# Scores as two full-row passes, one weight-product burst per head pair, and gate sums ahead of their matmuls, in a two-block transformer kernel on one core

## The chip, the cores and the metric

The kernel runs as one program on one core of a Trainium2 chip. The metric is the device time of one execution in microseconds; the kernel before takes 2135.71 us, the median of three runs (2135.44 to 2136.05). Everything is computed in 32-bit floats; a long linear product is made of three matmuls on operands split into a high part (rounded to TensorE's reduced 32-bit format, `F32R`) and a low part (the remainder).

## The reference

512 tokens of width 1024 pass through two blocks. The first block has two layers of: a norm, one wide projection, sparse attention, a short convolution branch, gates, and an MLP of width 4096. In the attention, an indexer scores all keys for each query with four small heads, the best 128 (`topk`) keys are kept, and eight heads of width 64 attend to those:

```python
logits = jnp.einsum('bthd,bsd->bths', iqb, ikf)                 # indexer, 4 heads of 64
score = jnp.einsum('bths,bth->bts', jax.nn.relu(logits), iwb) * IDX_SCALE
_, idx = lax.top_k(score, topk)
s = jnp.einsum('bthd,btkhd->bthk', qb, kg) * scale              # 8 heads of 64
p = jax.nn.softmax(s, axis=-1)
return jnp.einsum('bthk,btkhd->bthd', p, vg)
```

The second block has a dilated attention of eight heads of width 64 beside an mLSTM with four heads (whose input and forget gates are eight columns of the input projection, `ig` and `fg`), and a SwiGLU of width 2816. Its modulation vector comes from a small product with `c`.

## The kernel before, in words

Activations lie as features x tokens, in tiles of 128 x 512. `linear` (L188) makes an output tile from three matmuls per 128 input rows (L230 to L232): high weights by high input, high weights by low input, low weights by high input. `linear_tok` (L240, matmuls L260 to L262) is the same with tokens on the partitions. Weights are fetched by SyncE's queue in pieces of up to 1 MB, and each unit of 128 x 1024 is split by ScalarE (L171) and VectorE (L172), two units ahead of use (`Prog.run`, L56).

The program is a list of steps in the order written. Attention steps are spread between the pieces of a projection by `interleave` (L85): in the first block's layers between those of the second gate, in the second block between those of the mLSTM projections. From the written order each engine's own order is planned when the program is built: an instruction written earlier goes first if its inputs and buffers are there by the planner's estimate. An engine then executes its order strictly; on TensorE matmuls start in that order. All 128 x 512 intermediate tiles come from one pool of 60 buffers (`slot`, tag `g`, L123); TensorE's output banks are four for linear layers (`mm`), three for attention and small products (`at`), one for attention outputs (`ot`).

Attention runs over 16 units: four head pairs times four query tiles `i` of 128 (`attn_pieces`, L417). For step `t` it writes the scores of unit `t`, the transposes of unit `t - 1` and the weight product of unit `t - 2`; the operands of the next pair (`parts`, L400) are written at a pair's second unit.

- `scores` (L344): per head a bank gets two matmuls with (i + 1) x 128 columns, at least 256. The first (L350) uses all 128 rows: the high query part stands twice, and the key operand has high and low part one above the other, so it gives qh kh + qh kl. The second (L351) uses 64 rows: ql kh. VectorE then adds the bias and takes the maximum (L354), ScalarE takes exp (L359) and scales (L362).
- `transp` (L365): TensorE transposes the weights tile by tile (L370); VectorE copies the first head's out of the bank (L373), ScalarE the second's (L375).
- `product` (L378): for a query tile, (i + 1) x 2 matmuls (L385); the two heads use 64 columns of the array each. A full 32-bit product (no `F32R`) is two instructions per matmul in the trace, so L385 has 480 of them in three attentions.

The index scores (`iscore`, L580) are made of a full-row and a 64-row matmul in the same way (L587, L588), 12 in each of the first block's layers. The gate columns of the second block (`gates0`, L1005) are made in two parts: VectorE adds the high and low part of four input tiles (L1014), and four matmuls with 32 columns of the array each (L1016), one strip for each tile, follow; the second part adds to the first. The first part is written after six, the second after eleven of the 16 pieces of the V projection. `qk1` has four matmuls of that shape too (L963).

Of the kernel before, what the change touches and what calls it, by code (L numbers as in the profile page):

```python
# [15 lines left out]
P = 128  # L16
# [11 lines left out]
# columns of the packed vectors  # L28
# [10 lines left out]
# columns of the constants  # L39
# [8 lines left out]
class Prog:  # L48
    """A list of emission steps; weight units are fetched and split ahead of use."""
# [35 lines left out]
def interleave(a, b):  # L85
    """Spread the pieces of b evenly between the pieces of a."""
    out = []
    na, nb = len(a), len(b)
    j = 0
    for i, x in enumerate(a):  # L90
        out.extend(x)
        while j < nb and (j + 1) * na <= (i + 1) * nb:
            out.extend(b[j])
            j += 1
    while j < nb:
        out.extend(b[j])
        j += 1
    return out
# [3 lines left out]
def blocks_kernel(ctx: ExitStack, tc: tile.TileContext, a: dict, out: bass.AP, stop=None):  # L102
# [35 lines left out]
    # ---------------------------------------------------------------- constants  # L138
# [16 lines left out]
    # ---------------------------------------------------------------- weights  # L155
# [25 lines left out]
    def halves(ch):  # L181
        """Units of at most 256 columns over all K tiles of a chunk."""
# [5 lines left out]
    def linear(W, row0, kts, c0, widths, xs, evac, parts_=1):  # L188
        """Output tiles (features x tokens) of W[row0:, c0:].T @ x; pieces of emission items.

        kts: K tiles per step; widths: columns of each output tile; xs: K tile -> (hi, lo);
        evac(j, psum, tokens) is emitted after the last product of output tile j; parts_: the
        tokens go through the group in that many parts, one after the other.
        """
# [45 lines left out]
    def linear_tok(W, c0, xs, evac):  # L240
        """Output tiles (tokens x 512 features)."""
# [37 lines left out]
    # ---------------------------------------------------------------- shared state  # L279
# [9 lines left out]
    def prep(key, j, gcol, sq=True):  # L289
        """x_j * g in two parts, and its part of the sum of squares."""  # L290
# [18 lines left out]
    def rstd(key):  # L309
        """1/sqrt(mean + eps) of every token, on all partitions."""  # L310
# [10 lines left out]
    def refine(y, v, t):  # L321
        """One Newton step of y = v ** -0.5."""
# [15 lines left out]
    # ---------------------------------------------------------------- attention  # L338
    def attn_unit(pair, i, stacks, V, bias, O):
        """Steps of one (head pair, query tile): scores, transposed weights, product."""  # L340
# [3 lines left out]
        def scores():  # L344
            qs, ql, ks = stacks[pair]
            WM = max(W, 2 * P)
            for hh in range(2):
                r = slice(64 * hh, 64 * hh + 64)
                ps = atbank()
                pe.matmul(ps[:, :WM], qs[hh][:, i * P : (i + 1) * P], ks[hh][:, :WM], start=True, stop=False)  # L350
                pe.matmul(ps[:, :WM], ql[r, i * P : (i + 1) * P], ks[hh][r, :WM], start=False, stop=True)  # L351
# [13 lines left out]
        def transp():  # L365
            for hh in range(2):
# [9 lines left out]
                st["T", hh] = pt  # L376

        def product():  # L378
            if i == 0:
                S["ops"] = otbank()  # L380
            ops = S["ops"]
            for j in range(i + 1):
                for hh in range(2):
                    h = 2 * pair + hh
                    pe.matmul(  # L385
                        ops[64 * hh : 64 * hh + 64, i * P : (i + 1) * P],
                        V(j)[:, 64 * h : 64 * h + 64],
                        st["T", hh][:, j * P : (j + 1) * P],
                        start=j == 0,
                        stop=j == i,  # L390
                    )
            st.pop(("T", 0))
            st.pop(("T", 1))
            if i == NT - 1:
                O[pair] = hilo(ops)
                stacks.pop(pair)

        return scores, transp, product

    def parts(q32, k32):  # L400
        """Two-part operands of a head pair: per head [qh; qh] and [kh; kl] (or [kl; kh]), and ql."""
        qs = [slot(F32R), slot(F32R)]
        ks = [slot(F32R), slot(F32R)]
        ql = slot(F32R)
        qh = slot(F32R)
        act.copy(qh, q32)
        dve.tensor_sub(ql, q32, qh.bitcast(F32))
        for hh in range(2):
            r = slice(64 * hh, 64 * hh + 64)
            o = slice(64 - 64 * hh, 128 - 64 * hh)  # L410
            act.copy(ks[hh][r], k32[r])
            dve.tensor_sub(ks[hh][o], k32[r], ks[hh][r].bitcast(F32))
            act.copy(qs[hh][r], q32[r])
            act.copy(qs[hh][o], q32[r])
        return qs, ql, ks

    def attn_pieces(q, k, V, bias, O):  # L417
        """Software-pipelined pieces over all (pair, query tile)."""
# [7 lines left out]
        us = [attn_unit(a_, i, stacks, V, bias, O) for a_ in range(4) for i in range(NT)]  # L426
# [3 lines left out]
        for t in range(n + 2):  # L430
# [7 lines left out]
            if t >= 2:  # L438
                p.append(("do", us[t - 2][2]))
# [4 lines left out]
    # ================================================================ block 1  # L444
    START = [1, 1, 2, 4]

    def dma_in(chunks):
        def f():
            act.activation(small(1, "nm"), epsc, AF.Sqrt)
            # keeps the PE array busy, so that its clock is up when the first operands arrive  # L450
# [24 lines left out]
    def layer1(l, nextprep):  # L475
# [6 lines left out]
        # ---- indexer projections  # L482
# [3 lines left out]
        def evA(j, ps, cs):  # L486
            if j < 2:
                t = slot()
                rope(ps, P, [t])
                ql = slot(F32R)  # L490
                qh = slot(F32R)
                act.copy(qh, t)
                dve.tensor_sub(ql, t, qh.bitcast(F32))
                for hh in range(2):
                    qs = slot(F32R)
                    r = slice(64 * hh, 64 * hh + 64)
                    act.copy(qs[0:64], t[r])
                    act.copy(qs[64:128], t[r])
                    iq[2 * j + hh] = (qs, ql)
# [981 lines left out]
```

## Time and profile before

| | |
|---|---|
| median of three runs | 2135.71 us (2135.44 to 2136.05) |
| profiled execution, first to last instruction | 2133.5 us, 2.2 us under the median; no other time of that execution is given |
| TensorE busy | 2126.5 us (100%), 9944 matmul instructions |
| VectorE busy | 1250.9 us (59%) |
| ScalarE busy | 864.9 us (41%) |
| GpSimd busy | 1.6 us |
| DMA | 215.25 MB, mean 101 GB/s |
| granted TensorE clock | 1.000 of full speed over the span |

A row of the timeline gives the start in us from the start of the span, the length of the record, the engine, the line of the kernel, and what was done; consecutive instructions of one line are merged (x8). The shape `64*128 64x256` means 64 rows and 128 columns of the array, and an operand of 64 partitions and 256 columns. A matmul's record is longer than the distance to its successor, since matmuls are pipelined: pitches are read from starts. PEld are the weight loads, which run beside matmuls.

### The profile page before, as it was taken

How to read it: one execution, taken by the hardware profiler on the slowest of the kernel's cores; microseconds unless marked ns; L12 is line 12 of the kernel's file. 1: busy time of each engine (PE TensorE's matmuls, PEld its weight loads, DVE VectorE, ACT ScalarE, POOL GpSimd, SP SyncE). 2: the span in 40 equal slices, each digit the busy share in tenths (PEclk: the TensorE clock that was granted, in tenths of full speed). 3: DMA queues.
4: the chain of work that ended last, by engine and by line, in shares of the span. 5: the costliest groups of instructions: out<-in, count | busy, mean ns of one | idle time of the engine just before them, and what ended most of it. 6: DMA issues, size and time to landing. Idle time of an engine off the chain costs nothing.

```text
span 2133.5 us, 25023 instructions
## 1 busy us (share of the span) xinstructions
PE 2126.5 (100%) x9944; PEld 1708.4 (80%) x9944; DVE 1250.9 (59%) x2231; ACT 864.9 (41%) x1383; POOL 1.6 (0%) x7
## 2 busy tenths in 40 slices
PE   9999999999999999999999999999999999999999
PEld 7788768888888877886788888889777789888887
DVE  6898546553434569965567746567766456333333
ACT  5324664441322342237634322325377644232221
POOL 0000000000000000000000000000000000000000
PEclk9999999999999999999999999999999999999999
DMA  6222113222332222221135636352211112323221
GB/s 205 92 99 98 61 40 98 88 94 97 99 99 99 84 99 79 99 99 54 46 99 175 213 127 209 130 202 97 79 60 60 60 60 88 111 79 119 79 97 61
DMA packets 122148, 215.25 MB, mean 101 GB/s; under 512 B 5808, under 2 KB 30640, under 8 KB 122032
## 3 DMA queue, kind: packets, MB, share of 16 engines
q1 hardware_dynamic: 122032, 213.67, 29.7%
q8 instruction: 78, 1.28, 0.2%
q14 instruction: 38, 0.31, 0.0%
HBM read 211.55 MB, written 2.10 MB: 100 GB/s over the span
## 4 chain that ended last, share of the span: by engine, by line
PE 99%; DVE 0%; ACT 0%; issue 0%; ACTq 0%
PE mm L230 25%; PE mm L232 25%; PE mm L231 25%; PE mm L1318 4%; PE mm L1319 4%; PE mm L1320 4%; PE ot L385 2%; PE at L351 2%; PE mm L260 2%; PE mm L262 1%; PE at L370 1%; PE mm L261 1%; PE at L350 1%; PE at L1191 0%; PE at L588 0%; PE at L1199 0%
## 5 line engine op out<-in xcount | busy, mean ns | idle before, releaser
L230 PE MATMUL mm<-g,wh 128*128 128x512 f32 (+1 forms) x2400 | 923.1, 385 | 0.2 <-ACT g L866 0.2
L231 PE MATMUL mm<-g,wh 128*128 128x512 f32 (+1 forms) x2400 | 918.2, 383 | 0.0
L232 PE MATMUL mm<-g,wl 128*128 128x512 f32 (+1 forms) x2400 | 917.4, 382 | 0.0
L171 ACT CAST wh<-raw 128x1024 fp32r<-128x1024 f32 (+2 forms) x356 | 366.4, 1031 | 866.9 <-PE mm L231 669.5
L172 DVE TENSOR_TENSOR wl<-raw,wh 128x1024 fp32r<-128x1024 f32 (+2 forms) x356 | 424.8, 1194 | 453.4 <-ACT wh L171 449.7
L230 PEld LDWEIGHTS mm<-g,wh 128*128 128x128 f32 x2400 | 450.5, 188 | 97.0 <-issue 10.3
L232 PEld LDWEIGHTS mm<-g,wl 128*128 128x128 f32 x2400 | 450.8, 188 | 89.4 <-issue 2.8
L231 PEld LDWEIGHTS mm<-g,wh 128*128 128x128 f32 x2400 | 450.7, 188 | 88.4 <-issue 3.7
L1320 PE MATMUL mm<-g,wl 128*128 128x512 f32 (+1 forms) x384 | 142.6, 372 | 0.0
L1319 PE MATMUL mm<-g,wh 128*128 128x512 f32 (+1 forms) x384 | 142.5, 372 | 0.0
L1318 PE MATMUL mm<-g,wh 128*128 128x512 f32 (+1 forms) x384 | 142.2, 372 | 0.0
L286 DVE TENSOR_TENSOR g<-g,g 128x512 fp32r<-128x512 f32 x96 | 66.2, 690 | 49.9 <-ACT g L285 49.7
L285 ACT CAST g<-g 128x512 fp32r<-128x512 f32 x96 | 59.5, 621 | 58.0 <-DVE g L713 26.6
L1320 PEld LDWEIGHTS mm<-g,wl 128*128 128x128 f32 x384 | 72.3, 188 | 12.6
L1319 PEld LDWEIGHTS mm<-g,wh 128*128 128x128 f32 x384 | 72.3, 188 | 12.4
L1318 PEld LDWEIGHTS mm<-g,wh 128*128 128x128 f32 x384 | 72.1, 188 | 12.4
L746 DVE TENSOR_TENSOR x<-mm,x 128x512 f32<-128x512 f32 (+1 forms) x68 | 44.7, 657 | 56.6 <-PE mm L232 56.6
L809 DVE SCALAR_TENSOR_TENSOR g<-g,g 128x512 f32<-128x512 f32 x96 | 63.8, 687 | 11.0 <-DMA g<-w_ada 10.8
L739 ACT ACTIVATE g<-g 128x512 f32<-128x512 f32 x64 | 40.3, 630 | 72.3 <-DVE g L738 72.2
L359 ACT ACTIVATE g<-g,nm 128x128 f32<-128x128 f32 (+3 forms) x96 | 53.5, 558 | 17.2 <-DVE nm L354 15.6
L362 ACT ACTIVATE g<-g,rec 128x128 f32<-128x128 f32 (+3 forms) x96 | 49.8, 554 | 14.3 <-DVE rec L361 13.9
L607 DVE MAX8 m<-g 128x8 f32<-128x256 f32 (+2 forms) x96 | 53.3, 557 | 2.1
(232 smaller groups left out, 1638.2 us busy)
## 6 DMA issues: line engine op xcount, KB each, us to landing
raw<-w_in SPq DMA_DIRECT2D x53, 1024.0 KB, 5.0
raw<-w_mlp_up SPq DMA_DIRECT2D x32, 1024.0 KB, 5.4
raw<-w_mlp_down SPq DMA_DIRECT2D x32, 1024.0 KB, 5.0
g<-w_ada SPq DMA_DIRECT2D x96, 256.0 KB, 5.7
raw<-w_gate SPq DMA_DIRECT2D x11, 1024.0 KB, 5.2
raw<-w_up SPq DMA_DIRECT2D x11, 1024.0 KB, 5.3
raw<-w_down SPq DMA_DIRECT2D x10, 1024.0 KB, 4.9
raw<-w_mix_out SPq DMA_DIRECT2D x8, 1024.0 KB, 4.9
```

The lines of the kernel that those rows point to most:

```text
L171: act.copy(hi, raw)
L172: dve.tensor_sub(lo, raw, hi.bitcast(F32))
L230: pe.matmul(ps, wh, hi[:, cs], start=st, stop=False)
L231: pe.matmul(ps, wh, lo[:, cs], start=False, stop=False)
L232: S["pe"] = pe.matmul(ps, wl, hi[:, cs], start=False, stop=en)
L285: act.copy(hi, src)
L286: dve.tensor_sub(lo, src, hi.bitcast(F32))
L359: S["exp"] = act.activation(s[:, :W], s[:, :W], AF.Exp, bias=nmax, scale=-1.0, accum_out=den)
L809: dve.scalar_tensor_tensor(w, w, 1.0, S["cb", n2], op0=ALU.mult, op1=ALU.mult, accum_out=modp[:, n2, n : n + 1])
L1318: pe.matmul(ps, wh, hi[:, cs], start=s == 0 and k_ == 0, stop=False)
L1319: pe.matmul(ps, wh, lo[:, cs], start=False, stop=False)
L1320: pe.matmul(ps, wl, hi[:, cs], start=False, stop=s == 1 and k_ == 3)
```

## The change

Scores: `two_part` puts the high and low part of a query one above the other in one 128-row operand; `doubled` makes two key operands, the high part twice and the low part twice. Each score is then two 128-row passes of the same width, with the high and with the low key operand; the sum has the product of the two low parts besides. ScalarE copies, VectorE subtracts, and GpSimd copies the second half of the low key. A pair's operands are released after the scores of its last query tile. The index scores use the same two helpers.

Products: the transposed weights of a pair's four query tiles are kept (`PT`), and `product` is written once per pair, at the place where the last tile's stood, with all 20 matmuls.

Gates: `gates_in` writes the VectorE sums of a part after four and after eight pieces of the V projection; `gates0` writes all eight matmuls after fourteen. `qk2` of the keys moves from after eight pieces to after six.

Comments and one docstring were removed besides.

```diff
@@ -335,20 +335,21 @@
         for o in outs:
             dve.tensor_add(o, t[:rows], sh[:rows])
-    def attn_unit(pair, i, stacks, V, bias, O):
+    def attn_unit(pair, i, stacks, PT, V, bias, O):
         st = {}
         W = (i + 1) * P
         def scores():
-            qs, ql, ks = stacks[pair]
+            qs, ks = stacks[pair]
+            if i == NT - 1:
+                stacks.pop(pair)
             WM = max(W, 2 * P)
             for hh in range(2):
-                r = slice(64 * hh, 64 * hh + 64)
                 ps = atbank()
-                pe.matmul(ps[:, :WM], qs[hh][:, i * P : (i + 1) * P], ks[hh][:, :WM], start=True, stop=False)
-                pe.matmul(ps[:, :WM], ql[r, i * P : (i + 1) * P], ks[hh][r, :WM], start=False, stop=True)
+                for n in range(2):
+                    pe.matmul(ps[:, :WM], qs[hh][:, i * P : (i + 1) * P], ks[hh][n][:, :WM], start=n == 0, stop=n == 1)
                 s = slot()
                 nmax = small(1, "nm")
@@ -373,49 +374,56 @@
                 else:
                     act.copy(pt[:, :W], ps[:, :W])
-                st["T", hh] = pt
+                PT[pair, i, hh] = pt
         def product():
-            if i == 0:
-                S["ops"] = otbank()
-            ops = S["ops"]
-            for j in range(i + 1):
+            ops = otbank()
+            for i_ in range(NT):
+                for j in range(i_ + 1):
+                    for hh in range(2):
+                        h = 2 * pair + hh
+                        pe.matmul(
+                            ops[64 * hh : 64 * hh + 64, i_ * P : (i_ + 1) * P],
+                            V(j)[:, 64 * h : 64 * h + 64],
+                            PT[pair, i_, hh][:, j * P : (j + 1) * P],
+                            start=j == 0,
+                            stop=j == i_,
+                        )
                 for hh in range(2):
-                    h = 2 * pair + hh
-                    pe.matmul(
-                        ops[64 * hh : 64 * hh + 64, i * P : (i + 1) * P],
-                        V(j)[:, 64 * h : 64 * h + 64],
-                        st["T", hh][:, j * P : (j + 1) * P],
-                        start=j == 0,
-                        stop=j == i,
-                    )
-            st.pop(("T", 0))
-            st.pop(("T", 1))
-            if i == NT - 1:
-                O[pair] = hilo(ops)
-                stacks.pop(pair)
+                    PT.pop((pair, i_, hh))
+            O[pair] = hilo(ops)
         return scores, transp, product
+    def two_part(r, o, src):
+        t = slot(F32R)
+        act.copy(t[r], src)
+        dve.tensor_sub(t[o], src, t[r].bitcast(F32))
+        return t
+    def doubled(r, o, src):
+        kh, kl = slot(F32R), slot(F32R)
+        act.copy(kh[r], src)
+        act.copy(kh[o], src)
+        dve.tensor_sub(kl[r], src, kh[r].bitcast(F32))
+        nc.gpsimd.tensor_copy(kl[o], kl[r])
+        return kh, kl
     def parts(q32, k32):
-        qs = [slot(F32R), slot(F32R)]
-        ks = [slot(F32R), slot(F32R)]
-        ql = slot(F32R)
-        qh = slot(F32R)
-        act.copy(qh, q32)
-        dve.tensor_sub(ql, q32, qh.bitcast(F32))
+        qs, ks = [], []
         for hh in range(2):
             r = slice(64 * hh, 64 * hh + 64)
             o = slice(64 - 64 * hh, 128 - 64 * hh)
-            act.copy(ks[hh][r], k32[r])
-            dve.tensor_sub(ks[hh][o], k32[r], ks[hh][r].bitcast(F32))
-            act.copy(qs[hh][r], q32[r])
-            act.copy(qs[hh][o], q32[r])
-        return qs, ql, ks
+            qs.append(two_part(r, o, q32[r]))
+            ks.append(doubled(r, o, k32[r]))
+        return qs, ks
     def attn_pieces(q, k, V, bias, O):
         stacks = {}
@@ -423,7 +431,8 @@
                 stacks[pair] = parts(q.pop(pair), k.pop(pair))
             return ("do", f)
-        us = [attn_unit(a_, i, stacks, V, bias, O) for a_ in range(4) for i in range(NT)]
+        PT = {}
+        us = [attn_unit(a_, i, stacks, PT, V, bias, O) for a_ in range(4) for i in range(NT)]
         n = len(us)
         pieces = []
@@ -435,19 +444,19 @@
             if 1 <= t <= n:
                 p.append(("do", us[t - 1][1]))
-            if t >= 2:
+            if t >= 2 and t % NT == 1:
                 p.append(("do", us[t - 2][2]))
             for it in p:
@@ -487,26 +496,14 @@
                 t = slot()
                 rope(ps, P, [t])
-                ql = slot(F32R)
-                qh = slot(F32R)
-                act.copy(qh, t)
-                dve.tensor_sub(ql, t, qh.bitcast(F32))
                 for hh in range(2):
-                    qs = slot(F32R)
                     r = slice(64 * hh, 64 * hh + 64)
-                    act.copy(qs[0:64], t[r])
-                    act.copy(qs[64:128], t[r])
-                    iq[2 * j + hh] = (qs, ql)
+                    o = slice(64 - 64 * hh, 128 - 64 * hh)
+                    iq[2 * j + hh] = two_part(r, o, t[r])
             else:
                 t = slot()
                 rope(ps, 64, [t[0:64, :]])
-                for hh in range(2):
-                    ks = slot(F32R)
-                    r = slice(64 * hh, 64 * hh + 64)
-                    o = slice(64 - 64 * hh, 128 - 64 * hh)
-                    act.copy(ks[r], t[0:64])
-                    iq["k", hh] = ks
-                    dve.tensor_sub(ks[o], t[0:64], iq["k", 0][0:64].bitcast(F32))
+                iq["k"] = doubled(slice(0, 64), slice(64, 128), t[0:64])
                 iw = slot()
                 dve.tensor_mul(iw[0:4, :], ps[64:68, :], S["n", "rs"][64:68, :])
@@ -580,12 +577,9 @@
             def f():
                 W_ = (i + 1) * P
-                r = slice(64 * (h % 2), 64 * (h % 2) + 64)
                 ps = atbank()
-                qs, ql = iq[h]
-                ks = iq["k", h % 2]
-                pe.matmul(ps[:, :W_], qs[:, i * P : (i + 1) * P], ks[:, :W_], start=True, stop=False)
-                pe.matmul(ps[:, :W_], ql[r, i * P : (i + 1) * P], ks[r, :W_], start=False, stop=True)
+                for n in range(2):
+                    pe.matmul(ps[:, :W_], iq[h][:, i * P : (i + 1) * P], iq["k"][n][:, :W_], start=n == 0, stop=n == 1)
                 wc = iwc[0][:, 4 * i + h : 4 * i + h + 1]
                 if h == 0:
@@ -999,39 +993,42 @@
             return f
         G = {}
-        def gates0(part):
+        def gates_in(part):
             def f():
-                if part == 0:
-                    G["ps"] = atbank()
-                ps = G["ps"]
-                hs = [slot() for _ in range(4)]
+                G["h", part] = [slot() for _ in range(4)]
                 for c in range(4):
                     hi, lo = xs(4 * part + c)
-                    dve.tensor_add(hs[c], hi.bitcast(F32), lo.bitcast(F32))
+                    dve.tensor_add(G["h", part][c], hi.bitcast(F32), lo.bitcast(F32))
+            return f
+        def gates0():
+            ps = atbank()
+            for part in range(2):
+                hs = G.pop(("h", part))
                 for c in range(4):
                     pe.matmul(ps[32 * c : 32 * c + 32, :], C2["wg"][:, 4 * part + c, :], hs[c], start=part == 0,
                               stop=part == 1, tile_position=(0, 32 * c))
-                if part == 1:
-                    r = slot()
-                    act.copy(r, G.pop("ps"))
-                    G["r"] = r
-                    C2.pop("wg")
-            return f
+            r = slot()
+            act.copy(r, ps)
+            G["r"] = r
+            C2.pop("wg")
         gv = linear_tok(W, 1024, xs, evv(V))
         add(gv[:2])
         do(qk1("rk"))
-        add(gv[2:6])
-        do(gates0(0))
+        add(gv[2:4])
+        do(gates_in(0))
+        add(gv[4:6])
+        do(qk2("rk", k, C_KG))
         add(gv[6:8])
-        do(qk2("rk", k, C_KG))
-        add(gv[8:11])
-        do(gates0(1))
-        add(gv[11:])
+        do(gates_in(1))
+        add(gv[8:14])
+        do(gates0)
+        add(gv[14:])
         def gates1():
             ps = atbank()
```

## Rows read from the trace of the kernel before

**Rows 1.** The page, part 4: shares of the chain that ended last, by engine.

```profile
PE 99%; DVE 0%; ACT 0%; issue 0%; ACTq 0%
```

**Rows 2.** Timeline of TensorE, 226 to 231 us: start us, us of record, engine, line, what.

```profile
226.04 0.39 PE L230 MATMUL mm<-g,wh 128*128 128x512 f32 x1
...
228.76 0.28 PE L350 MATMUL at<-g,g 128*128 128x256 f32 x1
228.97 0.38 PE L351 MATMUL at<-g,g 64*128 64x256 f32 x1
229.28 0.38 PE L350 MATMUL at<-g,g 128*128 128x256 f32 x1
```

**Rows 3.** The same, 1455 to 1463 us, where the matmuls have 256 columns.

```profile
1455.00 0.28 PE L231 MATMUL mm<-g,wh 128*128 128x256 f32 x1
...
1456.20 0.28 PE L232 MATMUL mm<-g,wl 128*128 128x256 f32 x1
```

**Rows 4.** The same, 238 to 250 us, the start of a first-block attention.

```profile
239.71 0.43 PE L385 MATMUL ot<-g,g 128*64 128x128 f32 x2
240.08 0.50 PE L230 MATMUL mm<-g,wh 128*128 128x512 f32 x1
...
242.33 0.40 PE L350 MATMUL at<-g,g 128*128 128x512 f32 x1
242.66 0.49 PE L351 MATMUL at<-g,g 64*128 64x512 f32 x1
243.08 0.50 PE L350 MATMUL at<-g,g 128*128 128x512 f32 x1
243.51 0.50 PE L351 MATMUL at<-g,g 64*128 64x512 f32 x1
```

**Rows 5.** The same, 1667 to 1676 us, the end of the second block's attention.

```profile
1669.62 0.88 PE L385 MATMUL ot<-g,g 128*64 128x128 f32 x12
1670.43 0.50 PE L260 MATMUL mm<-wh,g 128*128 128x512 f32 x1
...
1671.69 0.40 PE L262 MATMUL mm<-wl,g 128*128 128x512 f32 x1
1672.02 1.09 PE L385 MATMUL ot<-g,g 128*64 128x128 f32 x16
1673.04 0.50 PE L260 MATMUL mm<-wh,g 128*128 128x512 f32 x1
1673.38 0.39 PE L261 MATMUL mm<-wh,g 128*128 128x512 f32 x1
```

**Rows 6.** TensorE by lines: shapes, xcount | busy us (union), mean ns | idle before.

```profile
L385 PE MATMUL ot<-g,g 128*64 128x128 f32 x480 | 48.8, 286 | 0.0
...
L351 PE MATMUL at<-g,g 64*128 64x256 f32 (+2 forms) x96 | 40.7, 424 | 0.0
...
L588 PE MATMUL at<-g,g 64*128 64x256 f32 (+2 forms) x24 | 10.5, 437 | 0.0
...
L1016 PE MATMUL at<-g,g 128*32 128x512 f32 x16 | 7.5, 605 | 0.0
```

**Rows 7.** The page, part 5: TensorE's weight loads of line 230.

```profile
L230 PEld LDWEIGHTS mm<-g,wh 128*128 128x128 f32 x2400 | 450.5, 188 | 97.0 <-issue 10.3
```

**Rows 8.** Timeline of TensorE, 1504 to 1506.5 us.

```profile
1504.65 1.06 PE L963 MATMUL at<-g,g 128*32 128x512 f32 x8
```

**Rows 9.** VectorE by lines and shapes, 1556 to 1675 us.

```profile
L412 DVE TENSOR_TENSOR g<-g,g 64x512 fp32r<-64x512 f32 x8 | 5.5, 686 | 0.2
```

**Rows 10.** Stretches: their us, busy us (x instructions) of PE, PEld, DVE, ACT, POOL, granted clock.

```profile
226.00:323.00 97.00, 97.00 (x510) 66.66 (x510) 49.72 (x142) 68.51 (x154) 0.00 (x0) 1.00 0.13 44
1556.00:1675.00 119.00, 119.00 (x621) 85.12 (x619) 73.59 (x205) 89.82 (x189) 1.05 (x2) 1.00 0.16 54
1560.00:1580.00 20.00, 20.00 (x86) 13.88 (x86) 11.93 (x40) 17.18 (x39) 1.05 (x2) 1.00 0.20 58
```

**Rows 11.** GpSimd by lines.

```profile
L1074 POOL MEMSET g<- 128x512 f32 x1 | 0.5, 529 | 148.2 <-PE ot L385 148.2
```

## Prediction

> **What bounds the kernel now.** I read the chain that ended last first: TensorE is 99% of it and nothing else reaches 1% [rows 1]. So there is no wait to remove; a change pays only where TensorE itself needs fewer nanoseconds for the same products. "Busy" cannot show that, because a record of a matmul is longer than the distance to the next one. I therefore read the timeline of TensorE by distances from start to start. In the plain stream, 12 steps take 2.72 us, 0.227 us each for 512 columns [rows 2]; for 256 columns ten steps take 1.20 us, 0.12 each [rows 3]. Against these two pitches every irregular place can be priced.
>
> They are irregular at one kind of place: where the shape of the used array changes. In a score, the full-row pass (L350, 256 columns) is followed by the 64-row pass (L351) after 0.21 us instead of 0.12, and the 64-row pass by the next full-row one after 0.31 [rows 2]. With 512 columns it is 0.33 into the 64-row pass (0.10 over the pitch), 0.42 out of it (0.19 over), and the first full-row matmul behind it takes 0.43, which is 0.10 more than a first entry at 0.33 [rows 4]. The excess hardly depends on the width. A weight product burst (64 columns of the array, L385) costs likewise: two instructions hold TensorE 0.37 us [rows 4], 12 hold it 0.81 and 16 hold it 1.02 [rows 5], so 0.21 per four and about 0.16 fixed, and 0.10 more where the number is not a multiple of four. Entering it costs 0.33 - 0.227 = 0.10, and the first matmul behind it 0.34 - 0.227 = 0.11 [rows 5].
>
> **The change part by part.**
>
> *Scores.* The 64-row passes are 96 (L351) and 24 (L588) [rows 6]. Each becomes a 128-row pass of the same width: the number of matmuls and their columns stay. What goes is 0.09 to enter, 0.19 to leave and 0.10 on the matmul behind, 0.38 us. 120 x 0.38 = **45.6 us**. All of it is on TensorE, hence on the path. That a 128-row pass behind a 128-row pass into the same bank runs at the plain pitch is what every linear layer shows [rows 2, 3].
>
> The Trainium skill speaks against this part: "TensorE: Matmul & The Clock Gate", Part 3 (Packing small matmuls), says that a weight load overlaps matmuls in flight only if its row group differs, and the new passes share all rows. By that rule each of the 120 would wait for its load of 188 ns [rows 7], 22.6 us less gain. The trace disagrees: full-row matmuls of 256 columns follow each other every 120 ns [rows 3], each with a load of its own that is longer than that [rows 7]. I keep 45.6.
>
> *Products.* The same 480 instructions (two per product in 32-bit floats) run today in 78 bursts, the first and last of which are shown [rows 4, 5]; written are 48, so the planned order splits them. They occupy 48.8 us [rows 6]; the records overhang their follower by 0.07 (1672.02 + 1.09 against 1673.04), so they hold TensorE 48.8 - 78 x 0.07 = 43.3 us. After, one burst of 40 per head pair, 12 in all: 0.16 + 10 x 0.215 = 2.31 each, 27.7 in sum. That saves 15.6. Of the 78 entries 61 come from a full-row matmul (the other 17 come straight from a 64-row pass and are in the part above): 49 fewer x 0.10 = 4.9. Matmuls behind a burst: 66 fewer x 0.09 (0.11, less for the short transposes) = 5.9. Together **26.4 us** if no burst is split. I don't expect that: today the last instructions of a burst often wait alone, because the two heads' transposed weights leave by different engines. One extra fragment per pair costs 0.36, or 0.46 with an uneven count: 12 x 0.42 = **5 us back**.
>
> *Gate sums.* The 16 instructions of L1016 occupy 7.5 us [rows 6] in six fragments, so 7.1 without overhang; with six entries (0.09) and six followers (0.11) 8.3. The other four-strip product of the kernel, L963, does eight in one burst in 1.06 - 0.07 = 0.99 us [rows 8], since four strips then run side by side. Sixteen as one burst: about 1.9, plus 0.2 for entry and follower. Saved: **6.2 us**. It needs the eight sums ready: the second four (0.7 us each at the price of a VectorE subtraction [rows 9]) are written six pieces of six 0.227 us matmuls ahead, 8.2 us, so yes.
>
> *What is added.* Per head pair ScalarE has six copies instead of seven, VectorE four subtractions instead of three and GpSimd two copies instead of none; each layer's index scores lose six ScalarE copies, gain one VectorE subtraction on balance and one GpSimd copy. VectorE: 12 x 0.69 = 8 us [rows 9], in stretches where it is busy 49.7 of 97 us and 73.6 of 119 [rows 10]: hidden. A GpSimd copy of 64x512 has no row; the lower bound is its fill of 128x512, 0.53 us [rows 11], which reads nothing; above, the nearest row is VectorE's 0.69 for this shape with two inputs [rows 9], and I put the upper bound at twice that, 1.4. I take 0.7, nearer to the row of the shape. A pair's operands are written three query tiles ahead of use (97/16 = 6.1 us each), so the 18 copies of later pairs are hidden at any such price. The six of three first pairs and the two of the index keys have little lead, at worst 8 x 1.4 = 11 us, at best nothing, where other products stand ahead; I take **1 us back**. This is a new wait: the second score pass waits for GpSimd, and every matmul behind it with it, since they start in order. The moved steps issue no DMA.
>
> *What is late next.* TensorE loses 32 x 0.38 + 8.8 = 21 us in each attention. The first then lasts 97 - 21 = 76 us and ScalarE's 68.5 us of work fill 90% of it; the third 98 us, 89.8 of work, 92% [rows 10]. It stays just under. But in 20 us windows it does not: 17.18 us of work [rows 10] meet 16.5 us of TensorE. For such places, and for buffers (below), I take **3 us back**.
>
> Sum: 45.6 + 26.4 + 6.2 - 5 - 1 - 3 = 69 us. The profiled span is 2133.5 us and 2.2 lie around it to the median of 2135.7 shown; nothing around it changes. 2135.7 - 69 = 2066.
>
> **Rivals.**
>
> 1. *ScalarE takes over in attention.* For: 90 to 92% is more than this engine shows anywhere in these stretches today (71 to 75%), and its steps form chains with VectorE and TensorE. Against: the gate projections between the steps need nothing of the softmax. If it fills only 85%, the first lasts 80.6 us in place of 76, the second, which is the same code, likewise, and the third 105.7 in place of 98: 17 us; at 80%, 33. The time is then 2083 to 2100.
> 2. *The bursts stay split.* The order between the engines is planned, not written; the 48 written bursts became 78. If a pair's 40 go in four fragments, 36 extra cost 36 x 0.42 = 15 instead of 5: 2076. That the planner also keeps the gates in pieces adds up to 6: 2082.
> 3. *Weight loads serialise* (the rule above, as a mechanism of this kernel: 120 loads of 188 ns [rows 7] uncovered): 2066 + 22.6 = 2089. Today's full-row stream leaves it little [rows 3].
> 4. *The other side: the pool of 60 buffers runs out.* The weights of four query tiles now wait for one burst: ten buffers instead of four, and two pairs' operands take 12 instead of ten. At the end of the second pair of a layer's attention I count 16 (inputs) + 4 (V) + 8 + 4 (gates) + 5 (norm) + 2 (outputs) + 12 + 4 (scores) + 10 = 65, over 60, where it was 57. Then a VectorE or ScalarE instruction waits for a buffer that only the product burst frees, and behind it on the same engine stand the splits of the next weights and the evacuation of TensorE's banks. One tile's chain from its score to its product takes 239.71 - 228.76 = 11 us [rows 2, 4]. If TensorE idled for that at three pair ends in each of three attentions, 99 us are lost and the time is 2165; it is slower from 69 / 9 = 7.7 us per end. Against: the burst itself needs no buffer, and gate-projection products already loaded cover about 5 us (24 matmuls).
>
> **How the numbers follow.** Forecast (most of the sum kept): 0.62, with its own range 2054 to 2074. Rival 1: 0.17. Rival 2: 0.12. Rival 3: 0.02. Rival 4 in full: 0.04; the 0.03 left lies between it and the others, near no change. Faster by over 0.2% (4.3 us, about what a measurement here can tell): 0.62 + 0.17 + 0.12 + 0.02 = 0.93; within it 0.02; slower 0.05. The lower end, 2052, is no loss at all with 5 us more than counted; the upper, 2092, takes in rivals 2 and 3 and half of rival 1.
>
> **What would show it.** Right: no 64-row matmul left; the second score pass starts 0.12 or 0.23 us behind the first; L385's successor in 12 to 24 bursts, a full one holding TensorE 2.3 us; one gate burst of 1.9 us; each layer's attention some 20 us shorter; the MLP stretches unchanged. Wrong: starts of matmuls several tenths late inside attention with a ScalarE or VectorE releaser (rival 1 or 4), product bursts in fours and sixes (2), or score passes at 0.19 over the pitch (3). The forecast falls if attention shortens by less than 12 us each.

## The result, and the profile after

The changed kernel takes 2069.82 us (median of four runs, 2069.42 to 2069.96), the kernel before took 2135.78 us beside it (2135.44 to 2136.05). The ratio is 0.969 (95% interval 0.968 to 0.971): 65.9 us faster, where 69 were forecast. The span of the profiled execution fell by as much, from 2133.5 to 2067.9 us. A second timing of the same kernel beside later experiments gave 2070.38 us (2069.80 to 2070.69); that is how closely two numbers of this text can be compared.

TensorE is still the bound. The chain that ended last, its shares by engine:

```profile
PE 97%; DVE 1%; ACT 1%; issue 0%; DMA 0%; POOL 0%; SPq 0%; POOLq 0%; DVEq 0%; ACTq 0%
```

It was 99% TensorE [rows 1]; VectorE and ScalarE now have 1% each. That is the first sign of waits that were not there. The groups of TensorE's and GpSimd's instructions (engine, operation, operands, count, busy us, mean ns; then TensorE's idle time before them and what ended it):

```profile
L352 PE MATMUL at<-g,g 128*128 128x256 f32 (+2 forms) x192 | 44.7, 339 | 0.8 <-POOL g L412 0.8
L371 PE MATMUL at<-kon,g 128*128 128x128 f32 x240 | 40.2, 274 | 2.1 <-DVE nm L355 2.0
L386 PE MATMUL ot<-g,g 128*64 128x128 f32 x480 | 32.3, 277 | 0.0
L1013 PE MATMUL at<-g,g 128*32 128x512 f32 x16 | 1.9, 599 | 0.0
...
L412 POOL CAST g<-g 64x512 fp32r<-64x512 f32 x26 | 18.1, 698 | 1151.2 <-DVE g L411 1151.2
```

and the weight loads of the score passes:

```profile
L352 PEld LDWEIGHTS at<-g,g 128*128 128x128 f32 x192 | 31.6, 188 | 8.0 <-DVE g L374 1.3 <-POOL g L412 1.2 <-DVE rec L362 0.5
```

All 192 score passes (L352) use 128 rows; no group of 64-row matmuls is left. The product (L386) is 32.3 us busy instead of 48.8, the gate sums (L1013) 1.9 instead of 7.5 [rows 6].

TensorE's timeline, from four places of the kernel after, in the order of time (first attention three times, then the gate sums; start, length of the record, what):

```profile
232.88 0.87 PE L352 MATMUL at<-g,g 128*128 128x384 f32 x4
233.59 0.40 PE L231 MATMUL mm<-g,wh 128*128 128x512 f32 x1
...
282.77 0.39 PE L232 MATMUL mm<-g,wl 128*128 128x512 f32 x1
283.09 2.40 PE L386 MATMUL ot<-g,g 128*64 128x128 f32 x40
285.43 0.79 PE L352 MATMUL at<-g,g 128*128 128x384 f32 x3
...
294.34 1.74 PE L386 MATMUL ot<-g,g 128*64 128x128 f32 x26
296.01 0.50 PE L230 MATMUL mm<-g,wh 128*128 128x512 f32 x1
...
297.70 0.40 PE L232 MATMUL mm<-g,wl 128*128 128x512 f32 x1
298.03 1.09 PE L386 MATMUL ot<-g,g 128*64 128x128 f32 x14
299.05 0.50 PE L230 MATMUL mm<-g,wh 128*128 128x512 f32 x1
299.38 0.39 PE L231 MATMUL mm<-g,wh 128*128 128x512 f32 x1
...
1501.40 1.92 PE L1013 MATMUL at<-g,g 128*32 128x512 f32 x16
1503.25 0.50 PE L260 MATMUL mm<-wh,g 128*128 128x512 f32 x1
```

- Four score passes of 384 columns hold TensorE 0.71 us, 0.18 each, with no step at either edge. Before, the steps around each 64-row pass came to 0.38 us [rows 2, 4].
- A whole product burst of 40 instructions holds it 2.34 us (285.43 - 283.09). A pair's product that is split, 26 and 14, holds it 1.67 + 1.02 = 2.69, and the second fragment has an entry (0.33 - 0.227 = 0.10) and a slower matmul behind it (299.38 - 299.05 = 0.33, 0.10 over) of its own: one extra fragment costs 0.35 + 0.20 = **0.55 us**, not 0.42. Both parts of this split have an uneven count (no multiple of four), so the 0.10 for it is paid twice; the prediction charged it at most once. There are 22 bursts, against 78 before.
- The 16 gate instructions are one burst of 1.85 us.

What TensorE waited for in the kernel after (engine and awaiting line, releaser, total us, times, longest):

```profile
PE at L371 <- DVE nm L355: 2.0, 3, 0.9
...
PE at L352 <- POOL g L412: 0.8, 1, 0.8
```

Neither line exists before. The first is read in the timeline at the end of the first attention's second pair:

```profile
261.77 0.69 DVE L403 TENSOR_TENSOR g<-g,g 64x512 fp32r<-64x512 f32 x1
...
262.48 0.68 DVE L411 TENSOR_TENSOR g<-g,g 64x512 fp32r<-64x512 f32 x1
...
262.88 1.74 PE L386 MATMUL ot<-g,g 128*64 128x128 f32 x26
263.20 0.69 DVE L403 TENSOR_TENSOR g<-g,g 64x512 fp32r<-64x512 f32 x1
263.30 1.06 POOL L412 CAST g<-g 64x512 fp32r<-64x512 f32 x1 [15.12 <-DVE g L411]
...
263.92 0.99 DVE L411 TENSOR_TENSOR g<-g,g 64x512 fp32r<-64x512 f32 x1
264.93 0.42 DVE L355 CUSTOM_DVE_ANT_0 g<-at,bias 128x256 f32<-128x256 f32 x1
265.04 0.61 POOL L412 CAST g<-g 64x512 fp32r<-64x512 f32 x1 [0.67 <-DVE g L411]
...
265.51 0.30 PE L371 MATMUL at<-kon,g 128*128 128x128 f32 x1 [0.89 <-DVE nm L355]
```

VectorE makes the next pair's operands (four subtractions, 3.1 us in a row) and only then the maximum (L355) that empties a score bank; TensorE's next transpose (L371) is released by that maximum and comes 0.89 us late. The burst before it is already in pieces there. The same happens at 974 us. The wait for GpSimd occurs once, at the start of the second block's attention.

### The profile page after: what moved, and what is told of

The parts are those of the page before. It is cut to its first block, busy times and chain, and to the rows that moved or that the text cites. A ratio compares the mean times of both kernels' runs of the same rounds, so it can differ in the third digit from the quotient of the medians.

```text
span 2067.9 us, 25080 instructions
## 1 busy us (share of the span) xinstructions
PE 2057.1 (99%) x9944; PEld 1700.7 (82%) x9944; DVE 1260.0 (61%) x2245; ACT 845.6 (41%) x1359; POOL 19.7 (1%) x33
## 4 chain that ended last, share of the span: by engine, by line
PE 97%; DVE 1%; ACT 1%; issue 0%; DMA 0%; POOL 0%; SPq 0%; POOLq 0%; DVEq 0%; ACTq 0%
PE mm L230 25%; PE mm L232 25%; PE mm L231 25%; PE mm L1315 4%; PE mm L1317 4%; PE mm L1316 4%; PE at L352 1%; PE mm L260 1%; PE mm L261 1%; PE mm L262 1%; PE ot L386 1%; PE at L371 1%; PE at L1188 0%; PE at L1196 0%; PE at L582 0%
## 5 line engine op out<-in xcount | busy, mean ns | idle before, releaser
L171 ACT CAST wh<-raw 128x1024 fp32r<-128x1024 f32 (+2 forms) x356 | 366.4, 1032 | 825.8 <-PE mm L231 648.6
L602 DVE MATCH_REPLACE8 g<-m,g 128x256 f32<-128x256 f32 (+2 forms) x96 | 52.1, 543 | 0.0
```

Of the source, the lines that this page charges most:

```text
L171: act.copy(hi, raw)
```

## The experiments

The expectations call the kernels by the names in the headings.

**The parts alone: e1_scores, e2_products, e3_gates.** Each is the kernel before with one of the three parts of the diff and nothing else.

> The kernel before with the score part of the change alone (attention and index scores as two 128-row passes, GpSimd copies included); weight products and gates as before. Theory (each change of the used array shape costs TensorE time, the rows themselves nothing): 120 passes x 0.38 us go, 45.6 us, less about 1 us of waits: 2090 to 2092 us. Where the 8 us that the whole change gives back (73.6 us of shape changes gone, 65.9 us gained) come from: if from the score part's own waits on GpSimd and VectorE, 2096 to 2098 here; if they arise only when all parts together make TensorE faster than ScalarE and VectorE feed it, 2090 to 2092. Rival (64-row passes are slow only in the way their weights load, and 128-row ones pay 188 ns each): 2112.

> The kernel before with the weight-product part alone (one written burst per head pair); scores and gates as before. In the planned order there are 26 product bursts instead of 78. Theory (0.16 + 0.10 + 0.10 us for each burst, 0.10 more for an uneven one): about 20 to 22 us gained, 2114 to 2116. Rival (the pool of 60 buffers, with ten held for transposed weights, makes VectorE or ScalarE wait and TensorE behind them): 3 to 6 us less gained, 2118 to 2121, and starts of matmuls near pair ends late with a VectorE releaser.

> The kernel before with the gate part alone (sums written ahead, eight matmuls together, key norm earlier). Theory: six fragments become one of about 1.85 us, 6.2 us gained: 2129 to 2130. Rival (the gain of a burst is that it no longer waits for VectorE's sums, not that fragments are joined): the same time, but then the pitch inside the six fragments of before would show waits of VectorE; the trace of before shows none over 0.3 us on TensorE there.

Measured, beside the kernel before at 2136.02 us: e1_scores 2093.54 (ratio 0.980, 0.979 to 0.982), e2_products 2116.81 (0.991, 0.990 to 0.993), e3_gates 2129.74 (0.997, 0.996 to 0.998). The gains are 42.5, 19.2 and 6.3 us, 68.0 in sum, against 65.9 together. The parts are not quite apart, because the planned order moves with each: e1_scores has 70 product bursts, not the 78 of before, and by the count used below for the products its bursts cost 1.9 us less. So 45.5 + 1.9 us were to be had there, and 4.9 of them are given back by the score part alone. e1_scores came 1.5 us short of the first theory's range, and gained more than the second theory (2096 to 2098) allows: its trace has the pair-end waits already (0.82 us at 270 and at 986 us) and the GpSimd wait (0.92 us at 1531), 2.6 us in sum, so they belong to the new operands and not to the longer life of the weights. e2_products came 0.8 us short of its range (2114 to 2116) and below the rival's; there TensorE has no wait that the kernel before hasn't, and its 26 bursts take it most of the way from 26.4 (14 extra at 0.55 are 7.7, which leaves 18.7). e3_gates is inside its range.

**e4_grouped: is it the change of shape that costs, or the 64 rows?** The kernel before, in which both heads' 128-row passes come first and then both 64-row passes.

```diff
-            for hh in range(2):
-                r = slice(64 * hh, 64 * hh + 64)
-                ps = atbank()
-                pe.matmul(ps[:, :WM], qs[hh][:, i * P : (i + 1) * P], ks[hh][:, :WM], start=True, stop=False)
-                pe.matmul(ps[:, :WM], ql[r, i * P : (i + 1) * P], ks[hh][r, :WM], start=False, stop=True)
+            pss = [atbank(), atbank()]
+            for hh in range(2):
+                pe.matmul(pss[hh][:, :WM], qs[hh][:, i * P : (i + 1) * P], ks[hh][:, :WM], start=True, stop=False)
+            for hh in range(2):
+                r = slice(64 * hh, 64 * hh + 64)
+                pe.matmul(pss[hh][:, :WM], ql[r, i * P : (i + 1) * P], ks[hh][r, :WM], start=False, stop=True)
...
```

> The kernel before, with one thing changed: in an attention score both heads' 128-row passes come first and then both heads' 64-row passes (two banks at once); the same matmuls, rows and columns. Theory (the change of shape costs, not the 64 rows): 96 runs of one 64-row pass become 48 to 60 runs of two, so 36 to 48 x 0.38 us go: 2117 to 2122. Rival (a 64-row pass is slow in itself): no change, 2135 to 2137. Second rival (two banks at once starve the three banks of attention): up to 5 us slower than 2136.

Measured: 2120.15 us (ratio 0.993, 0.991 to 0.994), 15.9 faster with the same passes. Of 96 64-row passes of the attentions 62 now stand in pairs, so 31 edges are gone. In its timeline one such pair:

```profile
251.55 0.40 PE L349 MATMUL at<-g,g 128*128 128x256 f32 x2
251.88 0.38 PE L352 MATMUL at<-g,g 64*128 64x256 f32 x2
252.19 0.50 PE L230 MATMUL mm<-g,wh 128*128 128x512 f32 x1
```

Two 64-row passes of 256 columns hold TensorE 0.31 us (252.19 - 251.88), as one does in [rows 2] (0.31 from it to the next): the second starts 3 to 4 ns behind the first; the two use opposite halves of the rows. So a pair saves an edge (0.38) and a pitch (about 0.15), 31 x 0.53 = 16.4. The theory's range was hit by luck in part: it counted 36 to 48 edges and no pitch, and 31 edges alone are 11.8 us. The rival, by which order doesn't matter, falls. But since a pair runs side by side, this time alone can't tell a change of shape from a fixed price of each 64-row pass that a pair pays once; no run has two 64-row passes on the same half in a row. For the change of shape speak the other steps: of the 0.38 us, 0.09 stand ahead of the 64-row pass and 0.10 behind the full-row matmul that follows it; all three parts are the same within 0.01 at 256, 384 and 512 columns; and the product bursts pay such edges per burst and not per instruction (40 in one burst hold TensorE 2.34 us).

**a_after, e9_gated: what does a fragment cost, and is it a wait in disguise?** e9_gated lets the first matmul of a burst be one on the last query tile's weights, and the other 19 matmuls (38 instructions) are ordered behind it, last tile first. a_after is the changed kernel again.

```diff
-            for i_ in range(NT):
-                for j in range(i_ + 1):
-                    for hh in range(2):
...
+            todo = [(i_, j, hh) for i_ in reversed(range(NT)) for j in range(i_ + 1) for hh in (1, 0)]
+            head = mm(*todo[0])
+            with tc.issue_after(head.ins):
+                for it in todo[1:]:
+                    mm(*it)
```

> The changed kernel itself, again, so that small differences of the other three are read on one chip. Every theory expects 2069 to 2070.5 us.

> As the changed kernel, but a pair's product starts with a matmul on the last query tile's weights (the head whose copy ScalarE makes), and the other 39 instructions may only be planned behind it: 15 planned bursts in place of 22. Theory (each fragment costs TensorE about 0.4 us at its edges, and that is what is left to gain): 7 fewer, 2.8 us less, and perhaps one of the two 0.95 us waits at the end of the second pairs: 2066 to 2067.5. Rival (fragments sit where TensorE would otherwise wait for the softmax, so that a held-back burst turns into a wait of the same length): 2069 to 2071.

Measured: a_after 2070.38, e9_gated 2066.18 us (2065.57 to 2066.58): 4.2 faster, with 15 bursts instead of 22. The pair that was split above is now whole:

```profile
297.50 2.40 PE L386 MATMUL ot<-g,g 128*64 128x128 f32 x40
299.84 0.50 PE L232 MATMUL mm<-g,wl 128*128 128x512 f32 x1
```

Matmul by matmul of the linear layers, e9_gated was already 0.6 us ahead of a_after before the first attention, so 3.8 us go with the 7 fragments, 0.54 each on average, near the 0.55 read from the timeline (two of the three pairs that stay split do so in 28 and 12, which saves the uneven counts there). The waits at the second pairs' ends stay (0.86 and 0.88 us). The rival, by which a whole burst turns into a wait, falls.

**e6_dve_sub, e9_dve: does GpSimd's share cost TensorE time?** VectorE makes the second half of the low key by its own subtraction; e6_dve_sub is the changed kernel with that, e9_dve is e9_gated with that.

```diff
-        nc.gpsimd.tensor_copy(kl[o], kl[r])
+        dve.tensor_sub(kl[o], src, kh[r].bitcast(F32))
```

> As e9_gated, and VectorE makes the second half of the low key parts by a subtraction of its own; GpSimd makes none: 13 planned bursts. Theory A (GpSimd's slow copies, 1.06 to 1.14 us beside a VectorE subtraction that then takes 0.99 us instead of 0.68, and the 0.75 us wait for one of them, cost TensorE time): 1 to 2 us less than e9_gated. Rival (VectorE has 0.68 us more per copy instead, two per pair, in front of the maximum that TensorE's next transposes wait for, so the wait at the pair's end grows from 0.95 to about 2 us): no faster than e9_gated, or up to 2 us slower.

> As the changed kernel, with VectorE's subtraction in place of GpSimd's copy and nothing else; the planned order then has 32 product bursts instead of 22. Theory (fragments): 10 more at about 0.4 us, less the 0.75 us wait for GpSimd: 2072 to 2074. Rival (GpSimd beside VectorE is the larger cost of what was given back): 2067 to 2069.

Measured: e9_dve 2070.09 us, 3.9 slower than e9_gated and 1.9 beyond even the rival's range; e6_dve_sub 2076.05, 5.7 slower than a_after and 2 us beyond the theory's range. TensorE's waits in e9_dve:

```profile
PE at L371 <- ACT g L363: 2.3, 1, 2.3
PE at L371 <- DVE nm L355: 2.2, 7, 0.5
```

The 2.3 us stand at 1605 us, the end of the third attention, where the planned order had no projection left to cover the last softmax; e6_dve_sub has 1.5 there, and 32 bursts. By the starts of the linear matmuls the third attention is where both lose, 4.9 us (e9_dve) and 5.8 us (e6_dve_sub); their first two attentions are 0.1 to 0.4 us shorter than with GpSimd's copies, and the pair-end waits there fall from 0.9 to 0.5 us. So neither run falls in a stated range, and the versions with GpSimd's copies are faster as a whole; but one edit changed the planned order in more places than the one meant, and what the copies or the contention of the two engines cost by themselves is not shown.

**e11_plain, e11_12: the two waits, each by its cause.** e11_plain is e9_gated with VectorE's subtraction for the first pair of each attention only. e11_12 besides writes the next pair's operands for one head at the pair's second query tile and for the other at its third.

```diff
-            if t < n and t % NT == 1 and t // NT < 3:
-                p.append(stack(t // NT + 1))
+            if t < n and t % NT in (1, 2) and t // NT < 3:
+                p.append(stack(t // NT + 1, t % NT - 1))
```

> As e9_gated (2066.2 us), except that of each attention's first pair the second half of the low key parts is made by VectorE's subtraction and not by GpSimd's copy; the planned bursts stay 15. Theory (TensorE waited 0.75 us for that GpSimd copy once, at the start of the second block's attention, and elsewhere the copies have lead): 2065.4 to 2066, too near to e9_gated for the time alone, so the trace decides: a gap of 0.15 us or less at that place in place of 0.75, and the same waits of 0.9 to 1.05 us at the ends of the second pairs. Rival (the contention of the two engines matters wherever it occurs): more than 1.5 us below e9_gated.

> As e11_plain, and the operands of the next pair are written in two steps, one head at the pair's second query tile and the other at its third. Theory (at the ends of the second pairs in the first block TensorE waits 0.95 us for a maximum that VectorE makes late, because four subtractions of the next pair stand in front of it): both waits fall below 0.4 us, 1.2 to 1.9 us gained, and two planned bursts more (17) give back 0.8 us: 2064.5 to 2065.5. Rival (the wait belongs to the softmax chain's length, whatever stands in front of it): the waits stay, 2066 to 2067.

Measured: 2066.09 and 2065.39 us (2065.06 to 2065.66; ratio to before 0.967, 0.965 to 0.969). In e11_plain the gap behind GpSimd fell from 0.75 to 0.15 us as expected, and a new one of 0.48 us at a transpose 11 us later, which the profile puts down to ScalarE's split of a weight unit (L171), took most of it back: by the starts of the linear matmuls the third attention is not shorter than in e9_gated (0.4 us longer). The time is 0.1 us above the theory's range and equal to e9_gated's. In e11_12 the pair-end waits are gone:

```profile
262.70 0.41 DVE L355 CUSTOM_DVE_ANT_0 g<-at,bias 128x256 f32<-128x256 f32 x1
...
262.91 0.61 POOL L421 CAST g<-g 64x512 fp32r<-64x512 f32 x1 [11.61 <-DVE g L417]
...
263.49 0.33 PE L371 MATMUL at<-kon,g 128*128 128x128 f32 x1
263.74 2.19 PE L386 MATMUL ot<-g,g 128*64 128x128 f32 x36
```

The maximum now stands ahead of the rest of the subtractions, and the transpose shows no wait. But in each of these two attentions the order has one fragment more (a pair's burst in 32 and 8): a wait of 0.87 us gone and about 0.55 us back, and by the starts of the linear matmuls 0.35 and 0.25 us are gained on e9_gated. The time, 0.7 us below e11_plain, is inside the range; the rival falls. e12_act below agrees: with fewer copies on VectorE it has no wait over 0.1 us at these two places either. This is the fastest version found: 5.0 us under the changed kernel (2070.38 in its second timing), though from e9_gated on the steps are near what a measurement can tell.

**e8_bufs54: was the pool of buffers near its end?** The changed kernel with `bufs=54` in place of 60.

> The changed kernel (2069.8 to 2070.4 us) with 54 buffers in the common pool in place of 60; 23 planned bursts instead of 22. Theory (the pool has room to spare and my count of 65 was wrong): 2069.5 to 2071.5. Rival (buffers bound the pair ends, as the prediction's fourth rival counted them): at least three waits of over 1 us more on TensorE with a VectorE or ScalarE instruction that waited for a buffer, 2074 us or more.

Measured: 2070.12 us, no change, with 23 bursts. TensorE's waits for the maximum fell rather than rose, and the planned order came out otherwise: the first two attentions, with one burst fewer each, are 0.7 to 0.8 us shorter than in a_after, and the third, with 13 bursts instead of 10, is 1.9 longer, so the equal time is a sum of both. The waits:

```profile
PE at L371 <- DVE nm L355: 1.2, 3, 0.5
PE at L352 <- POOL g L412: 0.8, 1, 0.8
```

A pool 11 below the prediction's count of 65 brings none of the long waits that the rival asks for: not all that I summed has to be held at one time. Which part hasn't was not tried.

**e12_act: was ScalarE near its end?** e9_gated with both heads' transposed weights copied by ScalarE.

```diff
-                if hh == 0:
-                    dve.tensor_copy(pt[:, :W], ps[:, :W])
-                else:
-                    act.copy(pt[:, :W], ps[:, :W])
+                act.copy(pt[:, :W], ps[:, :W])
```

> As e9_gated (2066.2 us), but ScalarE copies the transposed weights of both heads out of the banks and VectorE none: 16 copies of 0.41 us on average more per attention, 6.6 us, so ScalarE's work in the first one rises from 65.3 to about 72 us in 76 us; 14 planned bursts. Theory A (ScalarE, at 86 to 92% in these stretches, is close to taking over, as the prediction's first rival has it): TensorE gets waits of several us in each attention, 2070 to 2080. Rival (it still has room, since the gate projections between the steps need nothing of it): 2065 to 2067.5.

Measured: 2066.25 us, no change from 2066.18. The windows of the first and third attention in the changed kernel (length, then busy us of PE, PEld, DVE, ACT, POOL), then that of the first in e12_act:

```profile
226.00:302.00 76.00, 75.06 (x493) 61.82 (x492) 50.28 (x141) 65.30 (x151) 4.11 (x6) 1.00 0.17 56
1509.00:1607.00 98.00, 96.99 (x584) 78.15 (x583) 73.26 (x207) 80.09 (x176) 7.30 (x10) 1.00 0.20 65
```

```profile
226.00:302.00 76.00, 75.82 (x499) 62.16 (x499) 43.49 (x126) 70.26 (x167) 3.66 (x6) 1.00 0.17 56
```

ScalarE at 70.26 of 76 us (92%) still costs TensorE nothing that the time shows, inside the rival's range: the projections between the steps cover it.

## Why the prediction was right, step by step

- *Scores.* 45.6 forecast. Summed over the trace of before, the steps into, out of and behind 64-row passes are 45.5 us; none is left after. That the loads don't serialise shows after as well: 128-row passes of 256 columns follow each other 0.12 us apart (the median of 59 steps), and each of the 192 has a load of its own of 0.188 us.
- *Products.* 26.4 - 5 = 21.4 forecast. From the starts, the bursts with their entries and the matmuls behind them cost 56.9 us before and 37.0 after, of which 1.9 are the two pair-end waits: 21.8. Two sizes were off and cancelled: fewer fragments (10 instead of 12 extra), each dearer (0.55 instead of 0.42). That they met is luck.
- *Gates.* 6.2 forecast, 6.3 measured alone; one burst of 1.85 us where 1.9 was read off.
- *GpSimd.* A copy takes 0.61 us alone; the mean of the 26 is 0.70, the value taken. The first-pair waits were put at 1 us; one of three occurred, 0.75 us.
- *What is given back*, the mis-sized term: 1 + 3 = 4 us forecast besides the fragments; 45.5 + 21.8 + 6.2 - 65.7 (the last from the starts of the last linear matmul) = 7.8 measured. Of this 1.9 are the pair-end waits, 0.9 the GpSimd wait, 1.0 four shorter waits before transposes, and 0.1 lies ahead of any part of the change (0.4 in a_after): the first linear matmul starts 0.70 us later than before, but the fourth only 0.06. The other 3.9 us are spread over many short steps; their cause stays open. By e1_scores more than half of the 7.8 belong to the score part. The prediction looked for waits in ScalarE and in buffers; the largest that came were on VectorE, whose four subtractions stand ahead of the maximum at a pair's end. Its share of 50 of 76 us busy hid that.
- *Rival 1* (ScalarE takes over) did not occur. ScalarE fills 65.30 of 76 us and 80.09 of 98, 86 and 82%, where the prediction had 90 and 92 with the work of before; its 71 to 75% for before are means of whole attentions, and its own row of 20 us has 86%. e12_act shows no loss at 92% either. *Rival 2* (split bursts) occurred in part, most in the third attention, which has 10 of the 22 bursts for its four pairs: the planned order starts whatever is ready, and e9_gated shows what that costs. *Rival 3* did not occur. *Rival 4* did not occur, and 54 buffers were enough (e8_bufs54).
- "Each attention some 20 us shorter": by the starts of the linear matmuls 17.9, 17.9 and 14.7 us. The third is the one with 10 bursts and 1.5 us of waits.
- *The sum* is 69.2 before rounding, 2066.5 us; 3.3 us were missing, nearly all of them in what is given back.

## What to carry to other kernels

When one engine has nearly all of the chain, price its irregular places by the distance from start to start, not by busy time, and multiply by their count; here that gave the gain to 3 us in 66. In this kernel changes of the used array shape were paid per change, so passes of one shape belong together, in the written order and by an ordering constraint where a planner would fill gaps with fragments. What is moved off the bound engine is to be looked for in the order of the engine that takes it, at the point where the bound engine waits for that one's next result, and not in that engine's share of busy time.

## What the runs showed of the hardware that was not expected

- Two 64-row passes on opposite halves of the rows run side by side: two take 0.31 us, as one does, at 256 columns (e4_grouped).
- GpSimd's copies and VectorE's operations with both inputs in the on-chip memory hold each other up, and the one that starts second pays. Of the 26 copies of the kernel after 21 take 0.60 to 0.62 us; five take 0.98 to 1.14. Each of the five starts while such a VectorE operation runs (L403 or L1118) and ends 0.47 to 0.48 us after that one's end, as the copy at 263.30 above. A copy that starts first keeps its 0.61, and a subtraction that starts within it ends no earlier than 0.54 us after it: it takes 0.89 to 0.99 instead of 0.69 where it began 0.35 us or more before the copy's end, and 0.69 to 0.70 where it began in the copy's last 0.16 us:

```profile
245.57 0.61 POOL L412 CAST g<-g 64x512 fp32r<-64x512 f32 x1 [12.99 <-DVE g L411]
...
245.82 0.90 DVE L403 TENSOR_TENSOR g<-g,g 64x512 fp32r<-64x512 f32 x1 [0.39 <-ACT g L402]
```

  Beside operations that read one input from a bank (L355, L508, L661) a copy takes 0.61. The Trainium skill ("GPSIMD Engine Reference", 1. Specifications) says that GpSimd shares its interfaces to that memory with VectorE and contends with VectorE instructions that have two inputs there. The trace agrees, and gives the size: 0.4 to 0.5 us for a copy that comes second, 0.2 to 0.3 for a subtraction.
